# Transposed feed-forward products that walk the tokens in another order within an instruction

## The chip, the cores and the metric

The kernel runs on one core of one Trainium2 chip. The metric is device time in microseconds of one execution; two runs are given for the kernel before, and a profile of one execution.

## The reference

Two layers, each of a feed-forward, a token mixer and a second feed-forward, on 256 tokens of 1024 channels in float32. The change touches the two feed-forwards of each layer:

```python
def swiglu(x, w_gate, w_up, w_down):
    return (jax.nn.silu(x @ w_gate) * (x @ w_up)) @ w_down
...
for l in range(DEPTH):
    f = swiglu(x, ffn_w_gate[l, 0], ffn_w_up[l, 0], ffn_w_down[l, 0])
    x = layer_norm(ALPHA * x + 0.5 * f, ln_g[l, 0], ln_b[l, 0])
    z = x @ w_in[l]
    ...
    f = swiglu(x, ffn_w_gate[l, 1], ffn_w_up[l, 1], ffn_w_down[l, 1])
    x = layer_norm(ALPHA * x + 0.5 * f, ln_g[l, 2], ln_b[l, 2])
```

The hidden width is 2816, so gate and up have 22 column tiles of 128 each.

## The kernel before

All weights come from memory as 320 transfers of float32 blocks [128, 1024], most of them 512 KB. ScalarE copies each block into the type fp32r (the high part, `wh`), VectorE subtracts that from the raw block (the low part, `wl`); the activations are kept transposed, channels on partitions and tokens along the free dimension, as `xTh` and `xTl` ([8 row tiles, 256 tokens] each). A matrix product of exact parts is three passes: high by high, low by high, high by low, summed in PSUM.

A feed-forward works through units of its hidden columns (`ffn_units`). The first unit of the first feed-forward follows x as it arrives; in the other three feed-forwards two units ("nat") put the tokens on the partitions. All other units are "T": the weight tile [128, 128] is the stationary operand, the 256 tokens of one row tile of `xTh` or `xTl` are the moving one, and the output is [128 hidden columns, 256 tokens] in PSUM. `sub_T` does one column tile: 8 row tiles by three passes, 24 products of 256 columns. A full T unit is two gate and two up tiles, 96 products; the gate tiles share one bank (`pg`), the up tiles another (`pu`). ScalarE and VectorE then form silu and the product and split it into `hTh` and `hTl`. With `j` as the index of a unit, the first feed-forward has T units j = 1 to 10, the other three j = 2 to 11, of which j = 2 has one gate and one up tile. `sub_T` also does the column tiles of the mixer's input projection, from `col`.

`down` then multiplies `hTh`/`hTl` by the down weights, with 512 columns of the weights as the moving operand, and the layer norm follows.

Every instruction is recorded by `Program.add` with what it reads and writes, and issued by a greedy list schedule from costs written in the code (a product: `rhs.n / 2.4 + 2.3` ns); on TensorE it keeps the recorded order among those that are ready. All products are recorded in `mm`, so all of them carry one line, 308; transposes carry line 312, copies and activations 278, two-operand VectorE work 284.

Of the kernel before, what the change touches and what calls it, by code (L numbers as in the profile page):

```python
# [19 lines left out]
L = 2  # L20
DFF = 2816
KD = D // P
# [3 lines left out]

RING = 12          # split weight blocks on chip
RAW = 6            # raw weight blocks on chip
TAIL = 6           # row tiles of the down projection done half by half
TR0, TR1 = 4, 6    # where the normalized second half is transposed, in row tiles of the next products  # L30
TAIL_OUT = 6       # the same for the output projection
WARM = 4           # products of zeros that bring the tensor engine's clock up

# columns of the input projection
C_UV = 0
# [4 lines left out]
C_XR = 1792  # L40
# order of the transposed column tiles of the input projection
MIX_ORDER = ("xr0", "g2", "xr1", "g3", "xr2", "xr3", "c0", "x0", "c1", "x1", "b0", "b1")
MIX_BASE = {"xr": C_XR, "g": C_GATE, "c": C_C, "x": C_X, "b": C_B}
# order of the row tiles of the output projection: A, C, B
OUT_ROWS = (0, 1, 4, 5, 6, 7, 2, 3)

# per-channel parameters, [128, NPRM] per layer
PW = 0             # recurrent conv taps: sub * 4 + k
PB = 16            # recurrent conv bias
PBA = 20  # L50
PBI = 24
PLAM = 28
PS = 32            # short conv taps: sub * 3 + k
NPRM = 38


def ffn_units(layer, i):
    """(kind, first column, columns) in order. "first": by row tiles as x arrives, "nat": with tokens
    on the partitions, first half of the tokens first, while the other half is still normalized,
    "T": with columns on the partitions."""  # L60
    if layer == 0 and i == 0:
        head = [("first", 0, 256)]
    else:
        head = [("nat", 0, 256), ("nat", 256, 128), ("T", 384, 128)]
    done = sum(n for _, _, n in head)
    return head + [("T", c, 256) for c in range(done, DFF, 256)]


class Buf:
    """An on-chip buffer [128, *shape]; its tile exists once its phase is open."""  # L70

# [65 lines left out]
class Program:  # L137
    """Records instructions with what they read and write, then issues them in the order of a
    greedy list schedule: on each engine the instruction whose result is due first."""

# [120 lines left out]
def build(tc, a):  # L261
    nc = tc.nc
    V, A, G, T = nc.vector, nc.scalar, nc.gpsimd, nc.tensor
# [3 lines left out]

# [1 line left out]
    def ap(v, dtype=None):  # L269
        return v.ap(dtype) if isinstance(v, View) else v  # L270
# [34 lines left out]

    def mm(out, lhsT, rhs, start, stop, cost=None):
        cost = cost or rhs.n / 2.4 + 2.3
        pr.add("T", cost, [lhsT, rhs], [out], lambda: T.matmul(  # L308
            out=ap(out), lhsT=ap(lhsT), rhs=ap(rhs), start=start, stop=stop))

# [8 lines left out]

# [1 line left out]
    cbufs, opened = [], {}  # L321

    def buf(name, shape, dtype=F32, pool=None, **kw):
        b = Buf(name, shape, dtype, phase=opened.get(pool), **kw)
        (cbufs if pool is None else phases[pool]).append(b)
        return b
# [4 lines left out]
    def phase(name):  # L331
        """All of this phase's buffers take the memory of the phase before."""
        cell = ("phase", name)
        phases[name] = []
        prev = [c for n, c in opened.items()]
        opened[name] = cell

        def go():
            if stack:
                stack.pop().close()  # L340
            s = contextlib.ExitStack()
            p = s.enter_context(tc.tile_pool(name=name, bufs=1))
            for b in phases[name]:
                b.tile = p.tile([P, *b.shape], b.dtype, name=b.name)
            stack.append(s)
        pr.add("X", 0.0, [], [frozenset([cell, *prev[-1:]])], go)
# [5 lines left out]
    prm = buf("prm", (L, NPRM), grain=L * NPRM)  # L352
    der = buf("der", (L, 12), grain=12)                # 0.5 * b_a, 0.5 * b_i, -4 * softplus
    mhalf = buf("mhalf", (1,))
# [14 lines left out]
    def bank(*shape):  # L369
        b = bank_fifo.pop(0)  # L370
        return b.alias(shape) if shape else b
# [3 lines left out]

# [1 line left out]
    pos = {"blk": 0}  # L377
# [19 lines left out]

# [1 line left out]
    def mm_nat(acc, lh, ll, h, l, start, stop):  # L399
# [11 lines left out]

    def sub_T(out, blk):
        i = blk % RING
        for k in range(KD):
            ks = slice(k * P, (k + 1) * P)
            mm(out, wh[i][ks], xTh[k, :], k == 0, False)
            mm(out, wh[i][ks], xTl[k, :], False, False)
            mm(out, wl[i][ks], xTh[k, :], False, k == KD - 1)

# [4 lines left out]

# [1 line left out]
    class LN:  # L426
# [37 lines left out]

# [1 line left out]
    def down(lh, ll, n, tail, scale, eps, last, nxt):  # L466
# [38 lines left out]

# [1 line left out]
    def ffn(layer, i, ln_prev, nxt, mid=None):  # L507
# [12 lines left out]
        for h in range(2):  # L520
            for j, (_, c0, n) in enumerate(nat):
                acc = bank()
# [20 lines left out]
        for j, (kind, c0, n) in enumerate(units):  # L543
            if kind == "nat":
                continue
            f, m = c0 // P, n // P
            if kind == "first":
                first_unit(take(4), th, hh, hTh, hTl)
                continue
            b = take(2 * m)  # L550
            pg, pu = bank(2, S), bank(2, S)
            for q in range(m):
                sub_T(pg[q, :], b[q])
            act(th[:m, :], pg[:m, :], AF.Tanh, scale=0.5)
            stt(th[:m, :], th[:m, :], 1.0, pg[:m, :], ALU.add, ALU.mult)
            unbank(pg)
            for _ in range(2):
                if todo:
                    hT(*todo.pop(0))
            for q in range(m):  # L560
                sub_T(pu[q, :], b[m + q])
            tt(hh[:m, :], th[:m, :], pu[:m, :], ALU.mult)
            unbank(pu)
            split(hTh[f:f + m, :], hTl[f:f + m, :], hh[:m, :])
            if mid and j == 3:
                mid()
        return down(hTh, hTl, NF, TAIL, 4.0 * ALPHA, 16.0 * EPS, last, nxt)

    def first_unit(b, th, hh, hTh, hTl):
        """The first unit takes x and the weights row tile by row tile, as they arrive."""  # L570
        accs = [bank() for _ in range(4)]
        for k in range(KD):
            i = b[k // 2] % RING
            for j in range(4):
                cs = slice((k % 2) * 512 + j * P, (k % 2) * 512 + (j + 1) * P)
                out = accs[j][:S]
                mm(out, wh[i][cs], xTh[k, :], k == 0, False)
                mm(out, wh[i][cs], xTl[k, :], False, False)
                mm(out, wl[i][cs], xTh[k, :], False, k == KD - 1)
        for j in range(2):  # L580
            pg, pu = accs[j], accs[2 + j]
            act(th[j, :], pg[:S], AF.Tanh, scale=0.5)
            stt(th[j, :], th[j, :], 1.0, pg[:S], ALU.add, ALU.mult)
            tt(hh[j, :], th[j, :], pu[:S], ALU.mult)
            split(hTh[j, :], hTl[j, :], hh[j, :])
        for b in accs:
            unbank(b)

# [1 line left out]
    def mixer(layer, ln_prev, nxt):  # L590
# [181 lines left out]

# [1 line left out]
    def derive():  # L774
        for l in range(L):
            ts(der[l, 0:8], prm[l, PBA:PBA + 8], 0.5, None, ALU.mult)
            z = prm[l, PLAM:PLAM + 4]
            m, e, s, s2, q, w = [b.all for b in sp_b]
            # exp(-|lambda|)
            ts(m, z, -1.0, None, ALU.mult)  # L780
            tt(e, m, z, ALU.min)
            act(e, e, AF.Exp)
            # log1p(e) = 2 * atanh(e / (2 + e))
            ts(w, e, 2.0, None, ALU.add)
# [7 lines left out]
            tt(q, q, s, ALU.mult)  # L792
            # softplus(-lambda) = max(-lambda, 0) + log1p(exp(-|lambda|))
            ts(m, m, 0.0, -4.0, ALU.max, ALU.mult)
            stt(der[l, 8:12], q, -8.0, m, ALU.mult, ALU.add)

# [1 line left out]
    phase("x0")  # L798
# [42 lines left out]
def pack_weights(w_gate, w_up, w_down, w_in, w_out):  # L841
    blocks = []

    def nat(w):                       # [1024, n] -> n / 128 blocks of 1024 / n row tiles each
        n = w.shape[1]
        blocks.append(w.reshape(n // P, D // n, P, n).transpose(0, 2, 1, 3).reshape(-1, P, D))

    def sub(w):                       # [1024, 128] -> 1 block
        blocks.append(w.reshape(KD, P, P).transpose(1, 0, 2).reshape(1, P, D))
# [71 lines left out]
```

## Time and profile before

| what | value |
|---|---|
| time, median of 2 runs | 935.82 us (935.45 to 936.18) |
| span of the profiled execution | 933.5 us |
| TensorE busy | 917.6 us, 98% of the span |
| weight loads busy (overlap the products) | 848.8 us, 91% |
| VectorE busy | 601.5 us, 64% |
| ScalarE busy | 436.4 us, 47% |
| read from memory and written | 176.20 MB and 1.05 MB, 190 GB/s over the span |

The profile tells for each engine how long it was busy. On TensorE products overlap, so a product's own duration is longer than the step from one start to the next; for the price of a product one reads the starts in the timeline. The chain that ended last says which engine's work decides the end; the windows give each engine's busy time, and the granted clock as a share of full speed, in a chosen stretch.

### The profile page before, as it was taken

The numbers are of one execution on the slowest core, as the hardware profiler recorded it, in microseconds if no ns is written. First come the engines' busy times: TensorE is split into PE (matmuls) and PEld (weight loads), VectorE is DVE, ScalarE is ACT, GpSimd is POOL, SyncE is SP. The second block draws the span as 40 slices with busy tenths as digits, with TensorE's granted clock in tenths as the row PEclk, the third lists the DMA queues.
The fourth block names the chain that finished last, engine by engine and source line by source line (L and its number), as shares of the span: only waits on it lengthen the run. The fifth ranks groups of instructions, "written<-read, shape, count | busy, mean of one in ns | idle before, by whom it ended". The sixth has DMA issues, their size and how long they took to land.

```text
span 933.5 us, 15553 instructions
## 1 busy us (share of the span) xinstructions
PE 917.6 (98%) x6348; PEld 848.8 (91%) x6348; DVE 601.5 (64%) x813; ACT 436.4 (47%) x549; POOL 16.9 (2%) x33
## 2 busy tenths in 40 slices
PE   9999999989999999999999999999899999999996
PEld 8999998879989999988899999888798899999885
DVE  6996654477888665654695665546778876656415
ACT  6664443247645444443344444433476354444310
POOL 0000000000000000000000000000000000000000
PEclk9999999999999999999999999999999999999999
DMA  8996566476348665665386666654863586666401
GB/s 311 347 337 202 182 186 196 137 224 228 114 154 275 189 195 182 190 194 182 120 271 198 194 187 185 191 189 118 249 220 89 182 276 188 191 184 191 145 1 45
DMA packets 51910, 178.25 MB, mean 191 GB/s; under 512 B 6144, under 2 KB 7936, under 8 KB 51840
## 3 DMA queue, kind: packets, MB, share of 16 engines
q1 hardware_dynamic: 51840, 177.28, 59.3%
q8 instruction: 49, 0.80, 0.3%
q14 instruction: 21, 0.17, 0.0%
HBM read 176.20 MB, written 1.05 MB: 190 GB/s over the span
## 4 chain that ended last, share of the span: by engine, by line
PE 94%; DVE 2%; DMA 2%; ACT 1%; SPq 1%; issue 0%; POOL 0%; DVEq 0%; ACTq 0%
PE bank L308 92%; PE bank L312 1%; DMA bs<-sgu_bT 1%; SPq L318 1%; DMA wi<-rg_wi 1%; DMA raw<-w 1%; DVE xr L702 1%; DVE xn L296 0%; DVE ib L284 0%; ACT L278 0%; ACT e L278 0%; DVE ra L284 0%; DVE yTl L284 0%; POOL wT L625 0%; POOL rs L284 0%
## 5 line engine op out<-in xcount | busy, mean ns | idle before, releaser
L284 DVE TENSOR_TENSOR wl<-raw,wh 128x1024 fp32r<-128x1024 f32 (+1 forms) x320 | 386.5, 1211 | 241.9 <-ACT wh L278 241.0
L278 ACT ACTIVATE wh<-raw 128x1024 fp32r<-128x1024 f32 (+1 forms) x320 | 333.7, 1049 | 394.2 <-PE bank L308 278.1
L308 PE MATMUL bank<-xTh,wh 128*128 128x256 f32 x1456 | 408.5, 281 | 0.4 <-ACT wh L278 0.4
L308 PE MATMUL bank<-xTh,wl 128*128 128x256 f32 x1456 | 406.6, 279 | 0.3 <-DVE wl L284 0.2
L308 PE MATMUL bank<-xTl,wh 128*128 128x256 f32 x1456 | 406.4, 279 | 0.0
L308 PEld LDWEIGHTS bank<-xTh,wh 128*128 128x128 f32 x1456 | 273.7, 188 | 1.1 <-ACT wh L278 0.8
L308 PEld LDWEIGHTS bank<-xTh,wl 128*128 128x128 f32 x1456 | 273.7, 188 | 0.9 <-DVE wl L284 0.9
L308 PEld LDWEIGHTS bank<-xTl,wh 128*128 128x128 f32 x1456 | 273.8, 188 | 0.2
L308 PE MATMUL bank<-wh,hTh 128*128 128x512 f32 (+1 forms) x374 | 143.1, 383 | 0.0
L308 PE MATMUL bank<-wl,hTh 128*128 128x512 f32 (+1 forms) x374 | 143.1, 383 | 0.0
L308 PE MATMUL bank<-wh,hTl 128*128 128x512 f32 (+1 forms) x374 | 142.8, 382 | 0.0
L308 PEld LDWEIGHTS bank<-wh,hTl 128*128 128x128 f32 x374 | 70.3, 188 | 14.7
L308 PEld LDWEIGHTS bank<-wl,hTh 128*128 128x128 f32 x374 | 70.5, 188 | 14.6
L308 PEld LDWEIGHTS bank<-wh,hTh 128*128 128x128 f32 x374 | 70.3, 188 | 14.7
L308 PE MATMUL bank<-wl,xTh 128*128 128x256 f32 (+1 forms) x160 | 55.3, 346 | 0.0
L308 PE MATMUL bank<-wh,xTh 128*128 128x256 f32 (+1 forms) x160 | 55.3, 345 | 0.0
L308 PE MATMUL bank<-wh,xTl 128*128 128x512 f32 (+1 forms) x160 | 54.4, 343 | 0.0
L296 DVE SCALAR_TENSOR_TENSOR xn<-xn,bank 128x512 f32<-128x512 f32 (+1 forms) x25 | 16.6, 663 | 44.0 <-PE bank L308 44.0
L284 DVE TENSOR_TENSOR hh<-th,bank 128x512 f32<-128x512 f32 (+1 forms) x42 | 27.5, 656 | 18.7 <-PE bank L308 18.6
L308 PEld LDWEIGHTS bank<-wl,xTh 128*128 128x128 f32 x160 | 31.1, 194 | 3.9
L308 PEld LDWEIGHTS bank<-wh,xTh 128*128 128x128 f32 x160 | 30.8, 193 | 3.8
L308 PEld LDWEIGHTS bank<-wh,xTl 128*128 128x128 f32 x160 | 30.9, 193 | 3.6
(95 smaller groups left out, 511.8 us busy)
## 6 DMA issues: line engine op xcount, KB each, us to landing
raw<-w SPq DMA_DIRECT2D x312, 512.0 KB, 4.0
gB<-ln_g SPq DMA_DIRECT2D x6, 512.0 KB, 6.7
bB<-ln_b SPq DMA_DIRECT2D x6, 512.0 KB, 5.5
raw<-w SPq DMA_DIRECT2D x8, 256.0 KB, 5.0
x0t<-xT SPq DMA_DIRECT2D x8, 128.0 KB, 4.5
xn<-x SPq DMA_DIRECT2D x2, 512.0 KB, 6.4
out<-xn SPq DMA_DIRECT2D x3, 256.0 KB, 2.0
wT<-sgu_wT SPq DMA_DIRECT2D x2, 256.0 KB, 6.6
```

Source lines behind the costliest of these rows:

```text
L278: pr.add("A", cost, views(in_, scale, bias), [out], lambda: A.activation(out=ap(out), in_=ap(in_), func=func, scale=ap(scale), bias=ap(bias)))
L284: pr.add(eng, cost, [in0, in1], [out], lambda: e.tensor_tensor(out=ap(out), in0=ap(in0), in1=ap(in1, F32 if as32 else None), op=op))
L296: pr.add("V", cost, views(in0, s, in1), [out], lambda: V.scalar_tensor_tensor(out=ap(out), in0=ap(in0), scalar=ap(s), in1=ap(in1), op0=op0 ...
L308: pr.add("T", cost, [lhsT, rhs], [out], lambda: T.matmul(out=ap(out), lhsT=ap(lhsT), rhs=ap(rhs), start=start, stop=stop))
L312: pr.add("T", 109.0, [in_, ident.all], [out], lambda: T.transpose(out=ap(out), in_=ap(in_), identity=ap(ident.all)))
L318: pr.add("S", n, [], [out], lambda: e.dma_start(out=ap(out), in_=src), tail=2000.0, after=after)
L702: pr.add("V", 336.0, [ra[k, :], ib[k, :]], [xr[k, :]], lambda k=k: V.tensor_tensor_scan(out=ap(xr[k, :]), data0=ap(ra[k, :]), data1=ap(ib[ ...
```

## The change

`mm` gets an argument `order`. With an order (a, b, c), a * b * c = 256, both the moving operand and the output are viewed as `(a b c)` and walked as `b a c`: c neighbouring tokens from the first of a blocks, then c from the second, and so on through the blocks, then the next c of each block. A run is c columns of 4 bytes, the blocks start b * c columns apart. Every token's result lands at its own place in PSUM, so what is computed and what lies where stay as they are. `sub_T` hands the order on; in `ffn` the order of a T unit is entry `j % 12` of a table; the mixer's calls of `sub_T` have none.

```diff
+ORDERS = (None, (2, 32, 4), (32, 2, 4), (4, 16, 4), (16, 4, 4), (2, 16, 8), (2, 8, 16), (2, 4, 32), (2, 64, 2),
+          (128, 1, 2), (8, 8, 4), (64, 1, 4))
...
-    def mm(out, lhsT, rhs, start, stop, cost=None):
+    def walk(x, order):
+
+        if order is None:
+            return x
+        a, b, c = order
+        return x.rearrange("p (a b c) -> p b a c", a=a, b=b, c=c)
+
+    def mm(out, lhsT, rhs, start, stop, cost=None, order=None):
         cost = cost or rhs.n / 2.4 + 2.3
         pr.add("T", cost, [lhsT, rhs], [out], lambda: T.matmul(
-            out=ap(out), lhsT=ap(lhsT), rhs=ap(rhs), start=start, stop=stop))
+            out=walk(ap(out), order), lhsT=ap(lhsT), rhs=walk(ap(rhs), order), start=start, stop=stop))
...
-    def sub_T(out, blk):
+    def sub_T(out, blk, order=None):
...
-            mm(out, wh[i][ks], xTh[k, :], k == 0, False)
-            mm(out, wh[i][ks], xTl[k, :], False, False)
-            mm(out, wl[i][ks], xTh[k, :], False, k == KD - 1)
+            mm(out, wh[i][ks], xTh[k, :], k == 0, False, order=order)
+            mm(out, wh[i][ks], xTl[k, :], False, False, order=order)
+            mm(out, wl[i][ks], xTh[k, :], False, k == KD - 1, order=order)
...
+            order = ORDERS[j % len(ORDERS)]
             for q in range(m):
-                sub_T(pg[q, :], b[q])
+                sub_T(pg[q, :], b[q], order)
...
             for q in range(m):
-                sub_T(pu[q, :], b[m + q])
+                sub_T(pu[q, :], b[m + q], order)
```

The rest of the diff takes comments away, which shifts line numbers: line 308 becomes 319. No engine's instructions change places; only the shape of some products does. On TensorE, at the border between the units j = 7 and j = 8 of the first feed-forward, the program before has these rows (output, then the moving and the stationary operand, then the output's shape):

```order
L308 MATMUL bank_118<-xTh,wh_85 128x256
L308 MATMUL bank_118<-xTl,wh_85 128x256
L308 MATMUL bank_118<-xTh,wl_97 128x256
L308 MATMUL bank_119<-xTh,wh_86 128x256
L308 MATMUL bank_119<-xTl,wh_86 128x256
L308 MATMUL bank_119<-xTh,wl_98 128x256
```

The changed program has at the same place:

```order
L319 MATMUL bank_118<-xTh,wh_85 128x4x2x32
L319 MATMUL bank_118<-xTl,wh_85 128x4x2x32
L319 MATMUL bank_118<-xTh,wl_97 128x4x2x32
L319 MATMUL bank_119<-xTh,wh_86 128x64x2x2
L319 MATMUL bank_119<-xTl,wh_86 128x64x2x2
L319 MATMUL bank_119<-xTh,wl_98 128x64x2x2
```

The rows stand in the same order with the same operands. In the shape, the last number is the run, the one ahead of it the number of blocks, the one before that how often the walk goes round the blocks. Where the table's middle number is 1 the program keeps the plain shape 128x256.

## Rows read from the trace of the kernel before

**Rows 1.** The page: span, TensorE's busy time, share and instructions, granted clock by slice.
```profile
span 933.5 us, 15553 instructions
...
PE 917.6 (98%) x6348; PEld 848.8 (91%) x6348; DVE 601.5 (64%) x813; ACT 436.4 (47%) x549; POOL 16.9 (2%) x33
...
PEclk9999999999999999999999999999999999999999
```

**Rows 2.** The page: chain that ended last, shares of the span by engine and line.
```profile
PE 94%; DVE 2%; DMA 2%; ACT 1%; SPq 1%; issue 0%; POOL 0%; DVEq 0%; ACTq 0%
PE bank L308 92%; PE bank L312 1%; DMA bs<-sgu_bT 1%; SPq L318 1%; DMA wi<-rg_wi 1%; DMA raw<-w 1%; DVE xr L702 1%; DVE xn L296 0%; DVE ib L284 0%; ACT L278 0%; ACT e L278 0%; DVE ra L284 0%; DVE yTl L284 0%; POOL wT L625 0%; POOL rs L284 0%
```

**Rows 3.** The chain in order of time: start us, length us, what, instructions.
```profile
308.25 152.87 PE bank L308 x1063
...
495.59 152.87 PE bank L308 x1063
```

**Rows 4.** The page's groups, transposed products: busy us, mean ns | idle before.
```profile
L308 PE MATMUL bank<-xTh,wh 128*128 128x256 f32 x1456 | 408.5, 281 | 0.4 <-ACT wh L278 0.4
L308 PE MATMUL bank<-xTh,wl 128*128 128x256 f32 x1456 | 406.6, 279 | 0.3 <-DVE wl L284 0.2
L308 PE MATMUL bank<-xTl,wh 128*128 128x256 f32 x1456 | 406.4, 279 | 0.0
```

**Rows 5.** Timeline of TensorE inside a T unit: start us, length us.
```profile
319.75 0.28 PE L308 MATMUL bank<-xTl,wh 128*128 128x256 f32 x1
319.87 0.28 PE L308 MATMUL bank<-xTh,wl 128*128 128x256 f32 x1
319.99 0.28 PE L308 MATMUL bank<-xTh,wh 128*128 128x256 f32 x1
...
321.15 0.28 PE L308 MATMUL bank<-xTl,wh 128*128 128x256 f32 x1
```

**Rows 6.** Windows of 11.20 us, TensorE alone.
```profile
core 0: us, PE busy (x), PEclk, DMA share, GB/s
308.80:320.00 11.20, 11.20 (x99) 1.00 0.58 186
...
387.20:398.40 11.20, 11.20 (x99) 1.00 0.66 190
```

**Rows 7.** Timeline of TensorE in the down projection, first and last of 24 starts.
```profile
409.62 0.39 PE L308 MATMUL bank<-wh,hTh 128*128 128x512 f32 x1
...
414.99 0.40 PE L308 MATMUL bank<-wh,hTl 128*128 128x512 f32 x1
```

**Rows 8.** Timeline of TensorE in the mixer: f32 products of two records each.
```profile
226.22 0.59 PE L308 MATMUL bank<-xr,wa 128*128 128x256 f32 x2
226.65 0.59 PE L308 MATMUL bank<-xr,wi 128*128 128x256 f32 x2
...
229.88 0.59 PE L308 MATMUL bank<-xr,wa 128*128 128x256 f32 x2
230.31 0.60 PE L308 MATMUL bank<-xr,wi 128*128 128x256 f32 x2
```

**Rows 9.** VectorE's groups by form: busy us, mean ns | idle before.
```profile
L284 DVE TENSOR_TENSOR hTl<-hh,hTh 128x512 fp32r<-128x512 f32 x37 | 25.3, 684 | 0.0
...
L284 DVE TENSOR_TENSOR xTl<-bank,xTh 128x512 fp32r<-128x512 f32 x20 | 13.6, 690 | 2.1 <-ACT xTh L278 1.5
...
L284 DVE TENSOR_TENSOR hTl<-bank,hTh 128x256 fp32r<-128x256 f32 x6 | 2.5, 418 | 0.0
...
L284 DVE TENSOR_TENSOR hTl<-hh,hTh 128x256 fp32r<-128x256 f32 x5 | 2.1, 419 | 0.0
```

**Rows 10.** ScalarE's groups by form: busy us, mean ns | idle before, what ended it.
```profile
L278 ACT ACTIVATE wh<-raw 128x1024 fp32r<-128x1024 f32 x312 | 328.6, 1060 | 389.9 <-PE bank L308 278.1 <-issue 106.6 <-DMA raw<-w 5.3
...
L278 ACT ACTIVATE th<-bank 128x512 f32<-128x512 f32 x37 | 21.5, 580 | 6.0 <-PE bank L308 5.8 <-DVE hh L284 0.2
L278 ACT ACTIVATE xTh<-bank 128x512 fp32r<-128x512 f32 x20 | 11.8, 588 | 13.1 <-PE bank L312 12.9
```

## The prediction

> **What bounds the kernel now.** I read the page from the top. The profiled execution spans 933.5 us; TensorE is busy 98% of it, and its granted clock stands at the top digit in all 40 slices [rows 1]. The median of the two runs shown is 935.8 us, 2.3 us more than the span; I make the sum against the span and add those 2.3 us back at the end.
>
> Next the chain that ended last: 94% of it is TensorE, 92% of it the products recorded at line 308 [rows 2]. In order of time it is long unbroken pieces: from 308.25 us on, 1063 instructions in a row with nothing released from outside, 152.87 us; the piece from 495.59 us is the same [rows 3]. These pieces hold the transposed units of the feed-forward and most of the down projection behind them. So the reader is to see that nothing waits for data there: the time of such a stretch is the number of products times the spacing of their starts, and whatever a product's spacing gains or loses arrives at the end of the kernel in full.
>
> Then the products that the change touches. The page's groups list three passes of 1456 instructions of 256 columns each, 4368 in all [rows 4]. The mean of 280 ns there is a latency, not a price, because one product starts while the two before it are still in flight. The price is the spacing of starts: in the timeline 13 starts from 319.75 to 321.15 us, 12 steps in 1.40 us, **116.7 ns** [rows 5]. The windows say the same over whole units: a unit of two gate and two up column tiles has 4 x 8 x 3 = 96 products, 96 x 116.7 = 11.20 us; windows of 11.20 us show 99 products touched each (96 starts and those in flight at the edges) at a granted clock of 1.00, that is 2.4 GHz [rows 6]. So a column costs 116.7 / 256 = 0.456 ns.
>
> Two other rows say what kind of bound 116.7 ns is. The 512-column products of the down projection start every 233.5 ns (24 starts from 409.62 to 414.99 us, 23 steps) [rows 7], exactly twice as long: the price goes with the columns that stream, not with the instruction or with its weight load of 128 columns, which is the same in both. And the two-record f32 products of the mixer start 430 ns apart, 215 ns a record of 256 columns [rows 8]; a quarter of 430 is 107.5 ns, which is 256 columns at 2.4 GHz (106.7 ns) with hardly anything over. The fp32r products stand 9.2 ns above that. Something in streaming fp32r columns therefore already costs 9% over the clock, in every unit alike.
>
> **The change part by part.** Nothing is added, removed or moved between instructions: 6225 rows on TensorE before and after in the same order, the same reads, the same waits, and the planner's costs are unchanged. What changes is the address sequence inside a product, on the moving operand and on the output alike. Counting units: every feed-forward uses orders 3 to 8 and 10 once at full size (4 x 96 = 384 products each), order 2 with 96 + 3 x 48 = 240, order 1 with 96. The entries (128, 1, 2) and (64, 1, 4) have a middle size of one, so their walk is the contiguous one: for 384 + 288 products the change doesn't do what it says, and they are a control. Walked for real are 7 x 384 + 240 + 96 = **3024** products: 384 in runs of 2, 3 x 384 + 336 = 1488 in runs of 4, and 384 each in runs of 8, 16 and 32.
>
> A jump ends each run, so a product has 256 / run of them: 128, 64, 32, 16, 8. In all 384 x 128 + 1488 x 64 + 384 x (32 + 16 + 8) = 49,152 + 95,232 + 21,504 = **165,888 jumps**. The sum hangs on the price of one, and no row of TensorE shows a product with a broken walk, so I bound it.
>
> - Nothing: VectorE's low-part subtraction that writes hTl for the row-wise units walks two runs of 128 (tokens of one half, two column tiles) and takes 418 ns; the same subtraction over one unbroken run of 256 takes 419 ns [rows 9]. One jump more, no cost.
> - Something: the same operation over four runs of 128 takes 690 ns against 684 unbroken [rows 9], and ScalarE's copy into four runs 588 ns against 580 [rows 10]. Put wholly on the three jumps that is 2.0 to 2.7 ns each; 165,888 x 8/3 ns = 442 us, the far upper end. But source and function differ between these rows too.
> - Below nothing: if the other order happened to lift the 9.2 ns that fp32r pays over the clock, 3024 x 9.2 = 27.8 us would go.
>
> I take zero: the pair with the fewest differences (418 against 419) shows none, and every run starts on an even column and is whole pairs. A slower walk would have no cover: TensorE never waits inside these stretches, ScalarE already waits for it (278.1 us of idle time before the weight copies end on a product) [rows 10], and no later stage has idle time that an earlier surplus of weights could fill. A product that is not slower changes nothing else: the last product of a group still ends the same wait, and the bank is read whole afterwards.
>
> Sum: 933.5 + 0 + 2.3 = **935.8 us**.
>
> The Trainium skill speaks to this with two sentences of unlike strictness, on the page Advanced Engine Details and Errata, section Memory Cachelines. One says of PSUM that "Any non-contiguous AP significantly slows down matmuls"; by it all 3024 products would be slow, and that is the last rival below. The next asks only that every two consecutive elements be contiguous, and for SBUF the section asks for at least two hits on a 16-byte line; all runs here satisfy both, and by these the sum stays at 935.8 us. No row here shows either; I lean on the finer ones.
>
> **The rivals.** For a slowed product I use the only other warm rate of 256 columns in this trace, the f32 record's 215 ns, half the stream rate: 98.3 ns more.
>
> 1. *Only runs of two cost.* If columns are fetched or written in units wider than two, the shortest walk takes twice as many accesses and falls to half rate; the place is unit 8 of each feed-forward (2 blocks of 64 runs). 384 x 98.3 = 37.7 us, **973.5 us**. It counts as slower once these products lose 18.7 us / 384 = 49 ns each. For it: the 9% that fp32r already pays means the stream has no spare. Against: nothing shows a unit wider than a column.
> 2. *Each jump costs one column's time.* 165,888 x 0.456 ns = 75.6 us, **1011.4 us**; all walked units grow, in proportion to their jumps. It decides from 0.113 ns a jump. For it: the four-run rows; against it: the two-run pair.
> 3. *Runs of four or fewer at half rate*: (1488 + 384) x 98.3 = 184 us, **1119.8 us**, with units of runs of 8 to 32 untouched. It is rival 1 with a wider unit; the same rows speak for it and against it, and a full halving at runs of four needs a unit of eight columns.
> 4. *Any broken walk at half rate*: 3024 x 98.3 = 297 us, **1233 us**, all walked units at about 20.6 us and the two controls at 11.2. For it: TensorE has no row with a broken walk, so nothing excludes it; against it: neither VectorE nor ScalarE loses more than 8 ns in the broken walks they have. By the strict sentence of the skill's page above this is the case to expect.
> 5. *Faster*: the 9.2 ns are a collision of the straight walk with itself that other walks miss: 935.8 - 27.8 = **908.0 us**. The identical excess at 256 and 512 columns and in all units speaks more for a fixed rate than for a collision.
>
> **How the numbers follow.** No change 0.55; runs of two 0.13; a column a jump 0.10; runs of up to four 0.09; any walk 0.09; faster 0.04. About 2% (18.7 us) is what a measurement of this kernel can tell from no change; only the first case lies inside it. So faster 0.04, same 0.55, slower 0.13 + 0.10 + 0.09 + 0.09 = 0.41. The likeliest case by itself would be 933 to 940 us. The range has to leave out no more than 2 in 10: with the faster end, runs of two and a column a jump it holds 0.82, from 906 to 1013 us.
>
> **What would show it.** Right: starts 116.7 ns apart in every unit, the units of runs of 2 like those of 32, and the long pieces of the chain as long as now. Wrong: unlike spacings by shape. The trace keeps the shapes apart, so one table by unit tells the cases: only the 64x2 shape longer is rival 1; growth as 128 : 64 : 32 : 16 : 8 is rival 2; a step between runs of 4 and 8 is rival 3; all but the two controls is rival 4; spacing near 107 ns is rival 5. A growth that goes with the distance jumped instead of with the run (units with equal runs of 4 but 2, 4, 8, 16 or 32 blocks apart in price) would be something that none of my cases has.

## The result, and the profile after

The changed kernel takes 972.9 us (972.57 to 973.18), against 935.8: a ratio of 1.040, 95% interval 1.038 to 1.043. It is 37 us slower, inside the range but not where the forecast put it.

The page of the kernel after, its first lines (span, busy time and share of each engine), the granted clock by slice, and the first of the three groups of transposed products, which answer to [rows 1] and [rows 4]:

```profile
span 971.5 us, 15553 instructions
...
PE 954.8 (98%) x6348; PEld 886.0 (91%) x6348; DVE 601.3 (62%) x813; ACT 437.2 (45%) x549; POOL 15.8 (2%) x33
...
PEclk9999999999999999999999999999899999999999
...
L319 PE MATMUL bank<-xTh,wh 128*128 128x256 f32 x1456 | 422.4, 291 | 0.3 <-ACT wh L282 0.3
...
```

The reader is to see that nothing waits more than before: as many instructions, the same clock, the same idle time before the products. TensorE itself is busy 37.2 us longer (954.8 against 917.6), and the span is 38.0 us longer. The chain in order of time says it again; the piece of 1063 instructions that took 152.87 us [rows 3] is now

```profile
319.52 160.77 PE bank L319 x1063
```

Which products became dearer shows in windows cut at the first starts of the units j = 3 to 11 of the second feed-forward (columns as in [rows 6]):

```profile
core 0: us, PE busy (x), PEclk, DMA share, GB/s
312.60:325.76 13.16, 13.16 (x102) 1.00 0.59 192
325.76:336.78 11.02, 11.02 (x99) 1.00 0.54 190
336.78:348.62 11.84, 11.84 (x98) 1.00 0.58 179
348.62:360.14 11.52, 11.52 (x98) 1.00 0.63 183
360.14:371.54 11.40, 11.40 (x99) 1.00 0.61 185
371.54:388.17 16.63, 16.63 (x99) 1.00 0.43 135
388.17:399.38 11.21, 11.21 (x97) 1.00 0.53 175
399.38:411.29 11.91, 11.91 (x99) 1.00 0.56 177
411.29:422.49 11.20, 11.20 (x98) 1.00 0.57 189
```

Each window holds 96 products (and those in flight at its edges; the first has a few transposes of the row-wise units too). The two controls, the seventh and the last, stand at 11.20 us as before. The sixth, 2 blocks in runs of 2, takes 16.63 us, 173.2 ns a product; inside it the starts are 0.17 to 0.18 us apart:

```profile
371.69 0.35 PE L319 MATMUL bank<-xTl,wh 128*128 128x256 f32 x1
371.87 0.35 PE L319 MATMUL bank<-xTh,wl 128*128 128x256 f32 x1
```

And the second, 16 blocks in runs of 4, takes 11.02 us: that walk is *cheaper* than the straight one. From the starts of all units, with the products of each and their cost against 116.7 ns:

| blocks, run | ns from start to start | products | us in all |
|---|---|---|---|
| straight (and the two controls) | 116.7 | 672 | 0 |
| 2, 2 | 173.2 | 384 | +21.7 |
| 4, 4 | 133.3 | 384 | +6.4 |
| 8, 4 | 124.0 | 384 | +2.8 |
| 2, 8 | 123.3 | 384 | +2.6 |
| 2, 16 | 120.0 | 384 | +1.3 |
| 2, 4 | about 127 | 96 | +1.0 |
| 2, 32 | 118.7 | 384 | +0.8 |
| 32, 4 | 117.8 | 240 | +0.3 |
| 16, 4 | 114.8 | 384 | -0.7 |

The sum is 36.2 us, of the 37 to 38 us that are missing. So the account closes to 1 or 2 us from the prices of the products alone; what remained was why a walk has the price that it has.

### The profile page after: what moved, and what is told of

It is laid out like the page before. It is cut to its first block, busy times and chain, and to the rows that moved or that the text cites. A ratio compares the mean times of both kernels' runs of the same rounds, so it can differ in the third digit from the quotient of the medians.

```text
span 971.5 us, 15553 instructions
## 1 busy us (share of the span) xinstructions
PE 954.8 (98%) x6348; PEld 886.0 (91%) x6348; DVE 601.3 (62%) x813; ACT 437.2 (45%) x549; POOL 15.8 (2%) x33
## 4 chain that ended last, share of the span: by engine, by line
PE 94%; DMA 2%; DVE 2%; ACT 1%; SPq 0%; issue 0%; POOL 0%; DVEq 0%; POOLq 0%; ACTq 0%
PE bank L319 93%; PE bank L323 1%; DMA bs<-sgu_bT 1%; DMA raw<-w 0%; DVE xr L714 0%; SPq L329 0%; DVE xn L300 0%; DVE ib L288 0%; ACT L282 0%; ACT e L282 0%; DVE ra L288 0%; DVE yTl L288 0%; POOL wT L637 0%; POOL rs L288 0%; ACT wh L282 0%
## 5 line engine op out<-in xcount | busy, mean ns | idle before, releaser
L319 PE MATMUL bank<-xTh,wh 128*128 128x256 f32 x1456 | 422.4, 291 | 0.3 <-ACT wh L282 0.3
L319 PE MATMUL bank<-xTh,wl 128*128 128x256 f32 x1456 | 420.5, 289 | 0.3 <-DVE wl L288 0.2
L319 PE MATMUL bank<-xTl,wh 128*128 128x256 f32 x1456 | 420.5, 289 | 0.0
L319 PEld LDWEIGHTS bank<-wl,hTh 128*128 128x128 f32 x374 | 70.4, 188 | 14.5
L300 DVE SCALAR_TENSOR_TENSOR xn<-xn,bank 128x512 f32<-128x512 f32 (+1 forms) x25 | 16.6, 663 | 43.9 <-PE bank L319 43.9
```

Of the source, the lines that this page charges most:

```text
L300: pr.add("V", cost, views(in0, s, in1), [out], lambda: V.scalar_tensor_tensor(out=ap(out), in0=ap(in0), scalar=ap(s), in1=ap(in1), op0=op0 ...
L319: pr.add("T", cost, [lhsT, rhs], [out], lambda: T.matmul(out=walk(ap(out), order), lhsT=ap(lhsT), rhs=walk(ap(rhs), order), start=start, s ...
```

## The experiments

### Read side or write side

The change walks the moving operand and the output alike. The first two runs undo one side each.

```diff
-            out=walk(ap(out), order), lhsT=ap(lhsT), rhs=walk(ap(rhs), order), start=start, stop=stop))
+            out=ap(out), lhsT=ap(lhsT), rhs=walk(ap(rhs), order), start=start, stop=stop))
```

> The changed kernel with the walk on the moving operand alone; the output is written straight, so the tokens of the hidden columns come out permuted (that part of the computation is changed). In the changed kernel the steps from start to start by shape (blocks x run) are 173.2 ns for 2 blocks of runs of 2, 133.3 for 4 blocks and runs of 4, 124.0 for 8 and 4, 114.8 for 16 and 4, 117.8 for 32 and 4, 123.3, 120.0 and 118.7 for 2 blocks with runs of 8, 16 and 32, against 116.7 for the straight walk. Theory R (the price is paid where the columns are read): the same table again, time about 973 us. Theory W (it is paid where the results are written into PSUM): 116.7 ns in every unit, about 936 us. If both sides have a part: the table lies between, and what is missing here shows in the run with the output alone walked.

```diff
-            out=walk(ap(out), order), lhsT=ap(lhsT), rhs=walk(ap(rhs), order), start=start, stop=stop))
+            out=walk(ap(out), order), lhsT=ap(lhsT), rhs=ap(rhs), start=start, stop=stop))
```

> The changed kernel with the walk on the output alone; the moving operand is read straight, so the tokens of the hidden columns come out permuted (that part of the computation is changed). Theory R (read side): 116.7 ns in every unit, about 936 us. Theory W (write side): 173.2, 133.3, 124.0, 114.8, 117.8, 123.3, 120.0, 118.7 ns as in the changed kernel, about 973 us.

With the operand alone walked: 970.9 us, a ratio of 1.039 (1.034 to 1.043). Windows of the units 16 blocks by 4, 2 by 8 and 2 by 2, operand alone:

```profile
323.67:334.69 11.02, 11.02 (x99) 1.00 0.59 190
334.69:346.53 11.84, 11.84 (x98) 1.00 0.53 179
369.45:386.08 16.63, 16.63 (x99) 1.00 0.43 135
```

The same three lengths as in the changed kernel. With the output alone walked: 934.9 us, a ratio of 0.999 (0.998 to 1.000), and the units 16 by 4, 2 by 2 and the control:

```profile
312.91:324.11 11.20, 11.20 (x99) 1.00 0.59 187
357.71:368.91 11.20, 11.20 (x99) 1.00 0.57 187
368.91:380.11 11.20, 11.20 (x99) 1.00 0.61 189
```

Every unit at 11.20 us. Theory R stands, theory W falls: the whole price, the gain included, is paid where the moving operand is read; the output in PSUM adds nothing to a product in any of these orders.

### Length of the run, or distance

```diff
+ORDERS = {
+    (0, 0): (None, (2, 64, 2), (4, 32, 2), (8, 16, 2), (16, 8, 2), (32, 4, 2), (64, 2, 2), (2, 32, 4), (4, 16, 4),
+             (8, 8, 4), (16, 4, 4)),
...
-            order = ORDERS[j % len(ORDERS)]
+            order = ORDERS[layer, i][j]
```

> Both sides walked as in the change, but each feed-forward has a table of its own, so that 28 combinations of blocks and run are seen, six of them with runs of 2 (2, 4, 8, 16, 32 and 64 blocks). Theory L (the length of the run alone sets the price): all units with runs of 2 at 173 ns, all with runs of 8 at 123 ns; 12 units of runs of 2 cost 5.4 us each, with the rest about 1014 us. Theory D (the distance between blocks sets it: what collides is addresses that are a certain distance apart): runs of 2 spread by more than 20 ns between 2 and 64 blocks, with the lowest below 130 ns, as runs of 4 already spread from 114.8 (16 blocks) to 133.3 (4 blocks); about 950 to 1000 us.

It took 1061.8 us, more than either theory allowed. Windows of three units of the first feed-forward, runs of 2 over 2, 8 and 32 blocks:

```profile
17.59:34.22 16.63, 16.63 (x97) 1.00 0.97 358
56.24:78.00 21.76, 21.76 (x97) 1.00 0.50 170
98.91:121.31 22.40, 22.40 (x98) 1.00 0.37 117
```

That is 173, 227 and 233 ns. Over 4, 16 and 64 blocks it was 227, 218 to 221 and 229. With 2 blocks, which is what the change has, runs of 2 are thus the mildest of their kind; all others cost close to twice 116.7. Runs of 8 lay between 117 and 123 ns, of 16 between 118 and 120. Theory L fell (unlike prices at one length), and D fell too (no pair walk below 130 ns, and distance makes little of the step from run 4 to run 2). What the table suggests is a unit of four columns, 16 bytes: 233.3 is 128 of them at the 1.82 ns that 64 of them take in a straight product (116.7 / 64). That became theory F.

### Aligned pieces of 16 bytes

The next kernels take the one before and put groups of 48 products ahead of the units, which go into a bank that the unit's first product overwrites. One kernel so prices some fifty walks of the moving operand; only starts inside a group count, and each group's window below begins at its first start and is 48 steps long.

```diff
+    def walked(x, shift, dims):
...
+        p = x.ap[0]
+        return bass.AP(tensor=x.tensor, offset=x.offset + shift, ap=[list(p), *[list(d) for d in dims]])
...
+            bench((layer, i, j, 0), pg.root, b[0])
             for q in range(m):
                 sub_T(pg[q, :], b[q])
```

The list `dims` gives pairs of step and count, outermost first, and `shift` the first column.

> The kernel before, with 53 groups of 48 products put ahead of the gate or up tiles of a T unit; their results are overwritten and change nothing of what is computed, so only the steps from start to start inside each group count (the time grows by some 53 x 48 x 0.12 to 0.23 us). Theory F (the moving operand is fetched in aligned pieces of four columns, 16 bytes; a piece costs about 1.8 ns, a fetched piece is good only while the walk stays in it, and the pieces' distance adds some per cent): runs of 4 that begin two columns later straddle two pieces, so 128 pieces a product and 215 to 235 ns in place of 115 to 133; runs of 8 begun two columns later 96 pieces, about 175 ns; runs of 16 80 pieces, about 146 ns; the straight walk begun two columns later 65 pieces, 117 to 119 ns; pairs 4 columns or more apart 215 to 235 ns at any step; the same piece read 64 times over about 107 ns if it is kept. Theory L (the run's length in columns sets the price, wherever it begins): shifted and unshifted groups alike to 2 ns. For the order of whole pieces F forecasts only that steps stay within 107 and 135 ns.

Windows: straight; straight begun two columns later; 16 blocks by 4; the same begun two columns later; 2 by 8, and two columns later:

```profile
29.27:34.87 5.60, 5.60 (x50) 1.00 0.97 339
40.47:46.23 5.76, 5.76 (x50) 1.00 1.00 385
134.81:140.32 5.51, 5.51 (x50) 1.00 0.61 193
145.93:156.81 10.88, 10.88 (x51) 1.00 0.30 98
190.26:196.18 5.92, 5.92 (x50) 1.00 0.56 180
201.78:210.10 8.32, 8.32 (x51) 1.00 0.36 128
```

The same 256 columns in the same runs of 4 cost 114.8 ns where each run fills one aligned piece, and 226.7 ns where each lies across two. Runs of 8 go from 123.3 to 173.3 ns (forecast 175, for 96 pieces), of 16 from 120.0 to 150 (146, for 80). This is the run that theory L can't survive: length and jumps are equal, alignment alone differs. Misses of F: runs of 4 over 2 blocks, shifted, cost 173 and not 215 or more; the same piece read 64 times over costs 111.7, not 107; the straight walk begun two columns later 120.0, just above the 117 to 119; and the order of whole pieces matters more than the 107 to 135 ns that were forecast: steps of 64 and of 128 columns cost 146 ns, and one piece in every six (a step of 24 columns) 160 ns,

```profile
809.95:817.63 7.68, 7.68 (x51) 1.00 0.42 137
```

against 116.7 for one in three and 119.8 for one in two. All these walks use every piece whole, so a count of pieces alone doesn't give their prices.

The same method with other types and lengths:

```diff
+                if kind == "b":
+                    mov, sta = mov.bitcast(mybir.dt.bfloat16), sta.bitcast(mybir.dt.bfloat16)
+                    sta = walked(sta, 1, [[2, 128]])
```

> The same method: 35 groups of 48 products whose results are overwritten. Theory F (pieces of 16 bytes at 1.82 ns each, or 107 to 109 ns for 256 columns at the clock, whichever is longer): 256 columns of bf16 read straight are 32 pieces, 107 to 109 ns; every second bf16 element 64 pieces, 117 ns; every fourth 128 pieces, 215 to 235 ns; runs of 4 bf16 at a step of 8 (64 pieces) 117 ns; runs of 2 bf16 at a step of 8 (128 pieces) 215 to 235 ns; 512 bf16 straight (64 pieces) 213 to 216 ns by the clock. fp32r with 128, 192, 320, 384 and 512 columns 58, 88, 146, 175 and 233 ns, unless the weight load is longer. 512 columns of weights: 233 ns straight, 430 to 467 ns in runs of 2, 225 to 270 ns in runs of 4 to 16. Theory T (the 9% is a matter of the type fp32r, and the loss of short runs one of the number of jumps): all bf16 walks at 107 to 109 ns when straight or evenly stepped, whatever the step; fp32r as by F when straight.

Windows with bf16, 256 columns: straight (32 pieces); every second element (64); every fourth (128); runs of 8 at a step of 16 (32):

```profile
29.83:35.07 5.24, 5.24 (x51) 1.00 1.01 334
40.70:46.22 5.52, 5.52 (x51) 1.00 1.00 382
62.97:73.85 10.88, 10.88 (x51) 1.00 0.29 97
118.24:123.48 5.24, 5.24 (x51) 1.00 0.58 200
```

109.2, 115.0, 226.7 and 109.2 ns, and 226.7 too for runs of 2 at a step of 8 (128 pieces): with the type and the weights alike, the price follows the count of pieces and not the length of runs, as soon as it is over the clock's own time. Theory T falls. It also tells a good part of the 9.2 ns of the prediction: a straight fp32r product needs 64 pieces for 256 columns, and fetching 64 pieces takes longer than streaming 256 columns at 2.4 GHz; bf16, with half as many bytes a column, is at 109.2. One floor is separate: fp32r products of 128 and of 192 columns cost 111.7 ns each, not less, and so does a walk of 256 columns that stays in one piece and so has next to nothing to fetch. What these have in common is the load of 128 fp32r weights; that the load is the cause is not shown. Measured from that floor, the fetch accounts for 5.0 of the 116.7 ns. For the wide products the groups gave 233.2 ns straight, 461.5 in runs of 2 over 64 blocks, 327 over 2 blocks, 226.7 for 32 blocks by 4, and up to 279 for other runs of 4 (forecast 225 to 270).

### One part alone, and a version that gains

```diff
+ORDERS = (None, None, None, None, None, None, None, None, (2, 64, 2), None, None, None)
```

> One part of the change alone: the walk of 2 blocks in runs of 2 in unit 8 of each feed-forward, all other units straight. Theory F and any other that prices by unit: 4 x 96 products at 173.2 in place of 116.7 ns, 21.7 us, 957.5 us; the other walks together make the remaining 15 us of the change. A rival by which a slower unit is partly paid back later (the weight stream gets ahead) would show less than 21.7 us.

It took 956.9 us against 935.65 (ratio 1.022, 1.020 to 1.024): 21.3 us for 21.7 worked out from the steps. Within the interval, which leaves at most 3 us, nothing is paid back later; the rival in that expectation falls, and the sum over units holds.

```diff
+ORDERS = ((16, 4, 4),)
...
-            sub_T(b[:S], take(1)[0])
+            sub_T(b[:S], take(1)[0], ORDERS[0])
```

> All 4368 transposed products (the first unit and the mixer's column tiles too) walk 16 blocks in runs of 4, the one order that was cheaper than the straight walk: 114.8 against 116.7 ns. If that price holds everywhere: 4368 x 1.85 ns = 8.1 us less, about 927.8 us, 0.9% faster. If the gain was one of its neighbours in the changed kernel: 935.8 us.

926.4 us, a ratio of 0.990 (0.988 to 0.992), 9.3 us less than the kernel before beside it (8.1 forecast). The page shows TensorE's busy time 10.1 us lower than in [rows 1]:

```profile
span 924.3 us, 15553 instructions
...
PE 907.5 (98%) x6348; PEld 839.0 (91%) x6348; DVE 600.7 (65%) x813; ACT 436.4 (47%) x549; POOL 15.8 (2%) x33
```

Then a search over orders of whole pieces, rising and falling, and the same kind of order given to every product:

```diff
+    (0, 0, 3, 1): ('t', 252, [[-4, 4], [-16, 16], [1, 4]]),
...
+    (0, 1, 11, 0): ('n', 12, [[16, 32], [-4, 4], [1, 4]]),
+    (0, 1, 11, 1): ('n', 496, [[-16, 32], [4, 4], [1, 4]]),
```

> 53 groups of 48 products ahead of T units, results overwritten, each another order of whole 16-byte pieces: 256 columns of tokens (25 orders), 512 columns of weights (25), 256 columns of weights (3). Theory F with collisions (a piece costs 1.67 ns by the clock and some orders of pieces lose a few tenths of that to pieces that come too close after each other at certain distances): an order and its exact reverse cost the same to 1 ns (116.7 straight, 114.8 for 16 blocks of runs of 4), none is under the two floors that the last runs showed, 111.7 ns for any product of 256 columns or fewer with its weight load and 215.8 ns for 512 columns at the clock. If direction matters (pieces fetched ahead in rising order), reversed orders cost clearly more, up to double.

```diff
-        mm(acc, lh, h, start, False)
+        mm(acc, lh, h, start, False, order=(h.n // 16, 4, 4))
...
```

> A version meant to beat both kernels: every product of 256 columns walks 16 blocks in runs of 4, every product of 512 columns 32 blocks in runs of 4, both on operand and output. By the steps measured in single groups: 1422 wide products at 226.6 in place of 233.2 ns, 9.4 us under the version with the 256-column products alone (926.4), the 372 others 0.7 us: about 916 us, 2.1% faster than before. If the gain depends on which blocks are read (the groups read one block's first half): between 916 and 926 us.

In the search nothing went under the two floors, and nothing was better than 16 by 4 on 256 columns of tokens. But an order and its reverse are not alike: the windows show 16 by 4 and its exact reverse, then on 512 columns 32 by 4, a walk that rises with each four pieces reversed, the exact reverse of that walk, and straight.

```profile
29.42:34.93 5.51, 5.51 (x51) 1.00 0.90 324
62.88:68.53 5.65, 5.65 (x51) 1.00 0.55 187
485.02:495.90 10.88, 10.88 (x51) 1.00 0.28 96
635.53:648.33 12.80, 12.80 (x51) 1.00 0.25 82
653.93:665.13 11.20, 11.20 (x50) 1.00 0.29 95
975.92:987.12 11.20, 11.20 (x51) 1.00 0.29 95
```

114.8 against 117.7, and 266.7 against 233.3 ns: the forecast of prices equal to 1 ns failed, and so did that of a falling order being up to twice as dear, for the dearer one of the second pair is the one that rises as a whole. Which pieces come too close to which, if that is the reason, stays open.

The version with every product walked took 919.1 us, a ratio of 0.983 (0.981 to 0.985): faster than both kernels, by 1.7% (beside it) and 5.5% (against the 972.9 above), and 3 us short of the 916 forecast, within the 916 to 926 given for a gain that depends on the blocks read; which blocks, no run tells. First and last of 25 wide products in its down projection:

```profile
395.84 0.39 PE L318 MATMUL bank<-wh,hTh 128*128 128x512 f32 x1
...
401.29 0.38 PE L318 MATMUL bank<-wh,hTh 128*128 128x512 f32 x1
```

24 steps in 5.45 us, 227.1 ns against 233.5 in [rows 7].

### Why two blocks were milder

```diff
+    (0, 0, 3, 0): ('w', 0, [[0, 42], [4, 3], [1, 2]]),
+    (0, 0, 3, 1): ('w', 0, [[0, 32], [4, 4], [1, 2]]),
...
+    (0, 0, 9, 0): ('w', 0, [[2, 64], [128, 2], [1, 2]]),
```

> 27 groups of about 48 products ahead of T units, results overwritten; runs of 2 that come back to a few 16-byte pieces in turn. It asks why 2 blocks in runs of 2 cost 173 ns, three quarters of a full loss, while every further number of blocks costs 218 to 233. Theory H (some pieces are held, the oldest is given up): going round n pieces stays at the floor of 111.7 ns up to the number that is held and jumps to 210 to 235 ns beyond it; with two held, n = 1 and 2 are at 111.7 and n = 3, 4, 5, 8, 64 near 225. Theory P (a piece is kept by address only while it is the newest, and two in turn were cheap for another reason, such as the fetch of the next piece that runs ahead): no jump at a fixed n. For runs of 2 over 2 blocks 128, 256, 512, 1024, 132 and 144 columns apart: 173 ns at all distances if the number held decides, a spread of more than 20 ns if it is a collision of addresses; over 3 or 4 blocks 215 to 235.

Windows: going round 2, 3 and 4 neighbouring pieces in runs of 2; then runs of 2 over 2, 3 and 4 blocks (with 3 a product has 252 columns):

```profile
39.97:45.34 5.37, 5.37 (x51) 1.00 0.96 362
50.99:56.35 5.36, 5.36 (x50) 1.00 0.90 315
61.96:72.67 10.71, 10.71 (x51) 1.00 0.32 99
237.19:245.50 8.31, 8.31 (x51) 1.00 0.39 126
492.36:501.32 8.96, 8.96 (x51) 1.00 0.37 117
521.48:532.36 10.88, 10.88 (x50) 1.00 0.30 96
```

111.8 and 111.7, then 223 ns: up to three pieces are held, a fourth breaks it (theory H, with three where it guessed two; 5 to 64 pieces cost 220 to 229). With three it stays at 112 to 113 ns when the pieces lie 32 or 128 columns apart. So over 2 or 3 blocks the second half of a piece could be had without a new fetch, and 173 and 187 ns are less than the 227 over 4; why the second visit is cheaper but not free, 173 and not 117, this run doesn't settle.

Of the distance the walk over 2 blocks tells little. At 128, 256, 512 and 1024 columns apart it costs 173 ns each time, at 132 and 144 columns 164 to 166; but the same walk at 128 columns also took 166 in one half unit of the run on lengths, so 9 ns can't be put down to distance. Going round four pieces does depend on it: 223 ns for neighbours, 242 at 32 columns apart, 289 at 128, the last two above the 235 forecast. The window of the group at 32, then the group at 128 in two parts:

```profile
188.39:200.03 11.64, 11.64 (x51) 1.00 0.28 91
216.76:222.50 5.74, 5.74 (x22) 1.00 0.58 183
222.50:230.61 8.11, 8.11 (x29) 0.50 0.01 2
```

In the middle of the last group, after some 20 of its products, the granted clock falls from 2.4 to 1.2 GHz, and the step stays as it is, about 289 ns on both sides; the straight products behind it start about 214 ns apart until the clock is back. So the price of this walk does not hang on TensorE's clock, as one expects where the fetch is the bound.

## Why the prediction was wrong

**What bounds the kernel, and where a gain or a loss goes: right.** The time is the number of products times the step of their starts. The table of steps gives 36.2 of 37 to 38 us, and the run with the pairs alone 21.3 of 21.7.

**The price of a jump: wrong, and this is the step that failed.** "I take zero" rested on VectorE's pair of 418 against 419 ns [rows 9]. That row is of another engine, and its walk has two runs of 128 columns, with every piece used whole. The row that mattered was already there: 116.7 ns where the clock wants 106.7 [rows 5 and 8], in proportion to the columns [rows 7]. The prediction read from it that something costs 9% over the clock, called it a sign that the stream has no spare, and then still priced a broken walk by the engine that showed no loss. The runs showed in its place that the moving operand is fetched in aligned pieces of 16 bytes, at 1.7 to 1.8 ns a piece in the straight walk and in most walks that fetch pieces twice, and that a product bound by this fetch pays for what is fetched twice. Of the 36.2 us that the table gives, 21.7 are such a cost (unit 8, though its 173 ns in place of some 230 is only in part explained). The other 14.5 us fall on walks that use every piece whole, 64 a product: there the order of the pieces makes a fetch dearer, 133.3 / 64 = 2.1 ns over 4 blocks, and the reason for that stays open.

**The control units: right**, 11.20 us each.

**Rival 1, runs of two: its mechanism right, its place right, its time right by accident.** It forecast 973.5 us, with 37.7 us from runs of two and none from longer ones. Measured were 21.7 us from runs of two, probably because over 2 blocks part of the pieces is still held, and 14.5 us from longer runs, of which it knew nothing. Its half rate is real from 4 blocks on (218 to 233 ns).

**Rival 2, a price per jump: only in one family.** Over 2 blocks, runs of 32, 16, 8 and 4 lose 2.0, 3.3, 6.7 and 10 ns, roughly as their 8, 16, 32 and 64 jumps, at 0.16 to 0.25 ns a jump where the rival had 0.456. But 4, 8, 16 and 32 blocks by 4, all with 64 jumps, differ: +16.6, +7.3, -1.9, +1.1. The prediction's last sentence, a price that goes with the distance jumped and that none of its cases has, comes nearest, but it is no plain growth: 2 blocks, the farthest apart, lose less than 4.

**Rivals 3 and 4: fell.** No walk of 256 columns in whole aligned pieces cost more than 160 ns. For rival 4 the output alone walked cost nothing, and the read order of 16 by 4 gained. The strict sentence of the Trainium skill, Advanced Engine Details and Errata, Memory Cachelines, on any non-contiguous pattern in PSUM therefore doesn't hold for the outputs tried here (116.7 ns in every unit). The finer one for SBUF, at least two hits on a 16-byte line, was leaned on and misled: two columns a line are not enough for fp32r (218 to 233 ns over 4 and more blocks), nor for bf16 (226.7 ns with two a line, 115.0 with four). The line of 16 bytes itself the trace bears out.

**Rival 5, faster: wrong for the change, right as a mechanism in part.** About 5 of the 9.2 ns are the fetch, by the floor of 111.7 ns; 1.9 of these go with another order of the same pieces, and such orders are what the 919.1 us live on. It forecast all 9.2 ns and for every walk, and got 1.9 for one.

**The chances.** That the range holds 972.9 us is luck: it reaches so far for rivals 1 and 2, whose terms are not the ones measured. And 0.55 for no change was too much for a price that no row of the engine concerned showed, with one row that said the stream was at its limit.

## What to carry to other kernels

When an engine streams below its clock in proportion to what it streams, something that feeds it is the bound: count what it fetches, and expect a new access pattern to cost by that count first, not by what other engines lose in such a pattern; here the order of the pieces came on top and had to be measured. For a moving operand keep every run on whole aligned 16-byte pieces (four fp32r or eight bf16 columns), and don't begin short runs in the middle of one; in the straight walk that cost only 3.3 ns. Where the output lands in PSUM was free in every order tried, all with runs of 2 columns or more. Put an unknown price into the profile itself: one kernel with a different walk in each unit, or with groups of products that nobody reads, gave some fifty prices in one run.

## What the runs showed of the hardware that was not expected

- The moving operand is read in aligned 16-byte pieces: 256 columns of fp32r cost 114.8 ns in aligned runs of 4 and 226.7 ns in runs of 4 that begin two columns later.
- A product of 256 bf16 columns takes 109.2 ns when it touches 32 pieces, 115.0 with 64 and 226.7 with 128; a straight fp32r product, with 64 pieces, takes 116.7.
- Up to three pieces are held: going round three in runs of 2 costs 111.7 ns, round four 223 to 289, by their distance; the 289 ns stay when the granted clock falls from 1.00 to 0.50.
- An fp32r product of 128 or 192 columns costs about 111.7 ns from start to start, as much as one of 256 columns that stays in one piece.
- The order of whole pieces changes the rate between 114.8 and 160 ns for 256 columns, and is not the same for an order and its reverse; the rule behind it is open.
